# Four tiles for the attention's sums of x, an earlier copy of x into the output, and other banks at the borders of heads, in a one-core encoder block

## The chip, the cores and the metric

The kernel runs on one core of one Trainium2 chip. The metric is the device time of one execution in microseconds; the median of three runs is compared. PE is TensorE, DVE VectorE, ACT ScalarE, POOL GpSimd, SP the engine that issues nearly all DMAs. Numbers of lines (L748) are those of the kernel before.

## The reference

One encoder block on x of 1024 x 1024 (float32), with 16 learned meta tokens ahead of it:

```
u = rms_norm(h);  z = u @ w_in           # one projection, split into ten parts
branch A: bidirectional retention, 4 heads (dk 128, dv 256), chunks of 128,
          per-head norm, * silu(gate), @ w_ret_branch
branch B: windowed attention (+-128), 8 heads in 2 groups, rotary, meta keys,
          sink logit, * silu(gate), @ w_attn_branch
mix = sigmoid(g_r) * y_r + sigmoid(g_a) * y_a
out = h + rms_norm(mix @ w_out)          # meta rows dropped
```

## The kernel before

**Matmuls.** Every float32 product is three matmuls in the reduced type float32r: high times high, low times high, high times low (`mm3`, L79 to L81). Each operand is therefore split into a high part (a cast on ScalarE or GpSimd, `pool_hi` L92) and a low part (VectorE's subtraction `dve_lo`, L95). The large gate and branch products use a seven-product Strassen scheme (`Phase`), so sums and differences of quarters of x and of the weights are needed.

**Order of the work.** (1) Load x, split it, project q and k of head 0 (`qk0_mm`, over the k tiles), row squares of x on ScalarE (L377) for the norm; `normed` is the last of the instructions that make the row factors. `decay_table((h,))` (L248 to L250) makes head h's decay mask `DT`, with an exponential on ScalarE. (2) Four retention heads, `retention(h, fill)`: `stage1(c)` projects v of chunk c (`pv`), transposes k (`tr`) and makes the scores; `stage2(c)` makes the outputs of the forward scan (`pa`) and the states (`pkv`); then the backward scan runs over c from 8 down, with `finish(c)`, which transposes a normed output (`to`, L593), scales it on ScalarE into `ost` (L598) and stores it. (3) `attention()`: 32 chunks (2 groups, 16 blocks of 64 queries), `stage1` scores and softmax (`ps`, `p`), `stage2` transposes (`pt`), `stage3` values (`po`). (4) The phases z (gates), r and a (branch projections) and o (output projection, post norm, residual).

**What fills PE.** In a head's backward scan, `fill` takes steps of a list: the next head's q and k projection (`gen_qk`, 48 steps) and some steps of the "pre" products (`pe`, `gen_pre`; four steps make one product of 12 matmuls), namely (4, 4, 8) in heads 0, 1 and 2. There are seven fills of eight steps in such a head. A pre product (u, p) with p in `PRE[u]` is a product of phase z made ahead; its result goes to DRAM and is added in phase z. In the attention, `FILL[k]` gives how much of the remaining list is taken around chunk k, and `BEGUN` names, by the step of that list, helper work: loading and splitting weights (`half_w`, `pre_fetch`, `pre_sums`, `pre_parts`, `pre_low`) and the sums of x.

**Sums of x.** For eight steps q, `sum_fetch(q)` loads two tiles `xs` of 128 x 512 from x transposed (L748), `sum_scale(q)` scales them on ScalarE (L753), `sum_row(q)` forms four differences on VectorE in place (L760) and stores the two tiles to DRAM (L762). The two tiles are the only two buffers of their tag, so a step's fetch must wait for the store of the step before.

**Banks.** PSUM's eight banks are four groups: `pj` 3 (projections), `p1` 2 (`tr`, `to`, `rb`, `pt`), `p2` 2 (`pq` of head 0, `pkv`, `ps`), `p3` 1.

**The output.** Rows go out in tiles of 128. Rows 0, 1, 4 to 7 are added into `out` by an accumulating DMA of GpSimd, so x must lie there first: `x_to_out` copies x into `out` from DRAM to DRAM, 256 rows at a time, after chunks 4, 17 and 24 of the attention. Row tiles 2 and 3 come last; their x is loaded into SBUF (`xres`), added on VectorE (L1284), and a plain DMA on SP stores them. `final` is the last product, in two halves, each closed by `o_tail`.

**Scheduling.** The order within each engine is set by the framework from a simulated timeline; `tc.issue_after(i)` and `follow(...)` hold an instruction behind others.

Of the kernel before, what the change touches and what calls it, by code (L numbers as in the profile page):

```python
# [16 lines left out]
P = 128  # L17
KT = D // P
# [9 lines left out]
FILL = (((5, 4),) * 1 + ((5, 5),) * 1 + ((6, 4),) * 1 + ((4, 3),) * 1 + ((4, 5),) * 2 + ((4, 7),) * 1 + ((4,  # L28
        5),) * 1 + ((6, 4),) * 1 + ((5, 4),) * 1 + ((4, 3),) * 1 + ((4, 4),) * 1 + ((3, 5),) * 1 + ((4, 5),)
        * 1 + ((1, 4),) * 1 + ((6, 3),) * 1 + ((4, 5),) * 2 + ((4, 4),) * 1 + ((5, 4),) * 1 + ((3, 4),) * 1 +  # L30
        ((4, 3),) * 1 + ((4, 4),) * 2 + ((4, 2),) * 1 + ((4, 4),) * 1 + ((5, 4),) * 1 + ((3, 4),) * 1 + ((4,
        4),) * 1)
PRE = {u: (2, 3) if u > 5 else (2,) for u in range(2, 14)}
# [11 lines left out]
def block_kernel(ctx: ExitStack, tc: tile.TileContext, xT, x, meta, w_in, w_rb, w_ab, w_out, vecs, dec, sink,  # L45
# [106 lines left out]
    xm = wp.tile([P, KT, 2 * 32], R, name="xm")  # L152
# [45 lines left out]
    DT = ra.tile([P, NH, P], F32, name="DT")  # L198
# [69 lines left out]
    with tc.tile_pool(name="setup", bufs=1, reuse_waits="tile") as st:  # L268
# [119 lines left out]
    with tc.issue_after(rotated):  # L388
        decay_table((0,))
# [76 lines left out]
    def retention(h, fill):  # L466
# [122 lines left out]
        def finish(c):  # L589
            o = op[c - 1]  # L590
            to = p1(f"to{h}_{c}")
# [150 lines left out]
    def sum_fetch(q):  # L742

        k, c = q // 2, slice(256 * (q % 2), 256 * (q % 2) + 256)
        xsum[q] = {}
        for i in range(2):
            xsum[q][i] = t = aw.tile([P, 2, 256], F32, tag="xs", bufs=2, name=f"xs{i}{q}")
            nc.sync.dma_start(t, xT[4 * i + k, :, NM:T].rearrange("p (j t) -> p j t", j=2)[:, :, c])  # L748

# [114 lines left out]
    softmax, stored, last = [], [], {}  # L864
# [5 lines left out]
    with tc.issue_after(normed):  # L870
        evac_qk0(5)
    for h in range(NH):
        fill, drain = filler([gen_qk(h + 1), pieces(pre, (4, 4, 8)[h])] if h < 3 else [gen_ak(0), gen_ak(1), gen_aq(0, 0), gen_aq(0, 1), gen_aq(1, 0), gen_aq(1, 1)])
# [365 lines left out]
    rows, xres = {}, {}  # L1239
# [8 lines left out]
    def o_post(u, i, j, o, to=None):  # L1248
# [4 lines left out]
        if r not in rows:  # L1253
            rows[r] = (gp.tile([P, 3], F32, tag="ms2", bufs=4, name=f"ms2_{r}"), [], [])
            if u == 3:
                xres[i] = (lp if i else keep).tile([P, 4, 256], F32, tag="wr", bufs=2, name=f"xres{i}")
                xres[i] = xres[i].rearrange("p a b -> p (a b)")
                nc.sync.dma_start(xres[i], x[P * r:P * r + P])
# [3 lines left out]
        if u == 3:  # L1262
            nc.vector.tensor_tensor(to, o, pw[:, s], mul)
            o = xres[i]
# [14 lines left out]
    def o_out(r):  # L1279
        m2, parts, (m1,) = rows[r]  # L1280
        nc.gpsimd.tensor_tensor(m1, m1, mhalf[:, 0:1], ALU.pow)
        for s, to, o in parts:
            if r in (2, 3):
                nc.vector.scalar_tensor_tensor(to, to, m1, o[:, s], op0=ALU.mult, op1=ALU.add)  # L1284
                nc.sync.dma_start(out[P * r:P * r + P, s], to)
                continue
            nc.vector.scalar_tensor_tensor(to, o, m1, pw[:, s], op0=ALU.mult, op1=ALU.mult)
            nc.gpsimd.dma_start(out[P * r:P * r + P, s], to, accum_op=ALU.add)

    def o_tail(o, a):  # L1290
# [3 lines left out]
        nc.vector.tensor_tensor(o[:, s], o[:, s], pw[:, s], mul)  # L1294
        if a:
            parts.append((slice(0, 512), o, xres[1]))
# [53 lines left out]
    def attention():  # L1350
# [71 lines left out]
        def stage3(g, b):  # L1422
# [14 lines left out]
            if b % 2:  # L1437
                stored.append(nc.sync.dma_start(
                    oTa_d[4 * g:4 * g + 4, :, 64 * (b - 1):64 * (b + 1)].rearrange("e p t -> p e t"), oa[0]).ins)
# [55 lines left out]
        for k in range(len(chunks)):  # L1495
# [20 lines left out]
            if k in (4, 17, 24):  # L1516
                x_to_out({4: 0, 17: 4, 24: 6}[k])
# [6 lines left out]
             35: [(sum_scale, 3)], 37: [(sum_row, 3)], 40: [(sum_fetch, 4)], 45: [(sum_scale, 4)],  # L1524
# [124 lines left out]
```

## Time and profile before

| | |
|---|---|
| median of 3 runs | 1068.4 us (1066.32 to 1068.88) |
| the profiled execution | 1067.77 us, span 1066.0 us, mean granted clock 0.995 |
| PE busy | 1046.8 us (98%) |
| DVE, ACT, POOL busy | 849.2 (80%), 484.6 (45%), 212.4 (20%) |
| DMA | 190.36 MB, mean 179 GB/s |

The span runs from the first to the last instruction; the execution's own time is 1.8 us longer. A row of PE's waits names the instruction that waited, what it waited for, the total, the number of times and the longest. A row of windows gives busy time and started instructions of each engine in a stretch, then TensorE's granted clock (1.00 is full), the DMA engines' busy share and GB/s. In a timeline, `[0.61 <-ACT ost L598]` means that the engine was idle for 0.61 us before the instruction and what ended it. Matmuls overlap, so their times add to more than the span; counts per window are the better measure.

### The profile page before, as it was taken

The page shows a single profiled execution, that of the slowest core. Times are in us where ns is not written, and L with a number is a line of the kernel's source. Part 1 is how long each engine was busy: PE and PEld are TensorE (multiplying, and loading weights), DVE is VectorE, ACT ScalarE, POOL GpSimd, SP SyncE. Part 2 cuts the span into 40 slices and gives each one's busy share as a digit, 9 for nine tenths or more (in the row PEclk, how much of TensorE's full clock was granted, in tenths as well). Part 3 has the DMA queues.
Part 4 walks back from the last instruction along what each step waited for, and adds up shares of the span by engine and source line. Part 5 has one row for each costly group of instructions (what it writes and reads, how often), then busy time and mean ns, then how long its engine had stood idle before and what let it go on. Part 6 is the DMA issues. An engine that isn't in the chain of part 4 may idle for free.

```text
span 1066.0 us, 17137 instructions
## 1 busy us (share of the span) xinstructions
PE 1046.8 (98%) x5845; PEld 904.6 (85%) x5845; DVE 849.2 (80%) x1753; ACT 484.6 (45%) x1067; POOL 212.4 (20%) x270
## 2 busy tenths in 40 slices
PE   9999999999999999989999999999999999999997
PEld 7898999989998988877997888888888888787885
DVE  7787778768978548786768988998799799778765
ACT  5541442422411236565667545455456446333432
POOL 3324225134344224232210000000000000110032
PEclk9999999999999999999999999999999999999999
DMA  9321111203113427668668769899935746789464
GB/s 334 153 70 60 40 41 60 85 22 108 51 60 109 162 76 214 183 213 256 208 192 291 238 226 344 281 352 348 362 113 169 246 164 230 225 210 335 112 118 79
DMA packets 110632, 190.36 MB, mean 179 GB/s; under 512 B 11025, under 2 KB 50321, under 8 KB 109729
## 3 DMA queue, kind: packets, MB, share of 16 engines
q1 hardware_dynamic: 106944, 182.71, 51.4%
q0 software_dynamic: 3456, 6.29, 3.9%
q8 instruction: 46, 0.75, 0.3%
q14 instruction: 42, 0.34, 0.1%
q10 hardware_dynamic: 144, 0.27, 0.1%
HBM read 127.62 MB, written 62.40 MB: 178 GB/s over the span
## 4 chain that ended last, share of the span: by engine, by line
PE 94%; DVE 2%; DMA 1%; ACT 1%; issue 0%; SPq 0%; DVEq 0%; POOLq 0%; ACTq 0%
PE bz L80 8%; PE bz L81 8%; PE bz L79 8%; PE paq L80 3%; PE paq L79 3%; PE paq L81 3%; PE pv L79 3%; PE pv L81 3%; PE pv L80 3%; PE ba L80 2%; PE br L80 2%; PE br L79 2%; PE br L81 2%; PE ba L81 2%; PE ba L79 2%; PE bo L79 2%
## 5 line engine op out<-in xcount | busy, mean ns | idle before, releaser
L1232 POOL DMA_DIRECT2D mx_d<-c1a x4 | 3.7, 916 | 393.0 <-DVE c1a L1223 393.0
L81 PE MATMUL bz<-T,lhz 128*128 128x512 f32 x192 | 75.8, 395 | 0.0
L80 PE MATMUL bz<-T,llz 128*128 128x512 f32 x192 | 75.7, 394 | 0.0
L79 PE MATMUL bz<-T,lhz 128*128 128x512 f32 x192 | 75.2, 394 | 0.0
L79 PE MATMUL pv<-wh,big 128*128 128x256 f32 x256 | 73.0, 285 | 1.6 <-DVE vl L95 1.6
L80 PE MATMUL pv<-wh,big 128*128 128x256 f32 x256 | 73.1, 286 | 0.0
L81 PE MATMUL pv<-wl,big 128*128 128x256 f32 x256 | 73.0, 285 | 0.0
L80 PE MATMUL bz<-big,llz 128*128 128x512 f32 x176 | 69.7, 396 | 0.0
L81 PE MATMUL bz<-big,lhz 128*128 128x512 f32 x176 | 69.3, 394 | 0.0
L79 PE MATMUL bz<-big,lhz 128*128 128x512 f32 x176 | 68.8, 395 | 0.0
L1399 POOL TENSOR_SCALAR p<-p,den 128x352 f32<-128x352 f32 (+2 forms) x60 | 39.7, 674 | 107.7 <-DVE den L1392 82.8
L1389 ACT ACTIVATE p<-raw,nm 128x353 f32<-128x353 f32 (+2 forms) x64 | 36.1, 565 | 38.2 <-DVE nm L1386 37.9
L598 ACT ACTIVATE ost<-to,rnw 128x128 f32<-128x128 f32 x64 | 19.9, 364 | 73.2 <-PE to L593 58.3
L79 PE MATMUL paq<-big,wh 128*128 128x512 f32 x128 | 51.8, 405 | 0.0
L80 PE MATMUL paq<-big,wl 128*128 128x512 f32 x128 | 50.9, 398 | 0.0
L79 PEld LDWEIGHTS pv<-wh,big 128*128 128x128 f32 x256 | 48.9, 191 | 1.9 <-DVE vl L95 1.8
L81 PE MATMUL paq<-big,wh 128*128 128x512 f32 x128 | 50.4, 394 | 0.0
L81 PEld LDWEIGHTS pv<-wl,big 128*128 128x128 f32 x256 | 48.8, 191 | 0.1
L80 PEld LDWEIGHTS pv<-wh,big 128*128 128x128 f32 x256 | 48.8, 190 | 0.0
L80 PEld LDWEIGHTS bz<-T,llz 128*128 128x128 f32 x192 | 36.2, 188 | 8.5
L79 PEld LDWEIGHTS bz<-T,lhz 128*128 128x128 f32 x192 | 36.2, 188 | 8.4
L81 PEld LDWEIGHTS bz<-T,lhz 128*128 128x128 f32 x192 | 36.2, 188 | 8.4
(614 smaller groups left out, 3565.7 us busy)
## 6 DMA issues: line engine op xcount, KB each, us to landing
wrz<-in_w_in_dram SPq DMA_DIRECT2D x32, 512.0 KB, 6.0
wr<-in_w_in_dram SPq DMA_DIRECT2D x27, 512.0 KB, 4.0
e<-e SPq DMA_DIRECT2D x40, 256.0 KB, 4.8
we<-in_w_in_dram SPq DMA_DIRECT2D x16, 512.0 KB, 4.5
tg<-tg_d SPq DMA_DIRECT2D x32, 256.0 KB, 5.1
T<-preT SPq DMA_DIRECT2D x6, 1024.0 KB, 7.5
xt<-in_x_dram SPq DMA_DIRECT2D x8, 512.0 KB, 9.2
oTr_d<-ost SPq DMA_DIRECT2D x16, 256.0 KB, 2.1
```

Of the source, the lines that this page charges most:

```text
L79: nc.tensor.matmul(o, ah, bh, start=first, stop=False, **kw)
L80: nc.tensor.matmul(o, al, bh, start=False, stop=False, **kw)
L81: latest[:] = [nc.tensor.matmul(o, ah, bl, start=False, stop=last, **kw).ins]
L598: nc.scalar.activation(ost[0][:, e_, w0:w0 + P], to[:, P * e_:P * e_ + P], AF.Copy, scale=rnw[:, 2 * h + e_:2 * h + e_ + 1])
L1232: nc.gpsimd.dma_start(d, to, accum_op=ALU.add)
L1389: last["exp"] = nc.scalar.activation(p[:, 0:1 + wid], raw[e_][:, 0:1 + wid], AF.Exp, scale=-1.0, bias=nm_[:, e_:e_ + 1], accum_out=den[:, ...
L1399: nc.gpsimd.tensor_scalar(pt[e_][:, 0:wid], pt[e_][:, 0:wid], den[:, e_:e_ + 1], 1.0, op0=ALU.mult, op1=ALU.mult)
```

## The change

- **Sums of x.** Even steps keep the two `xs` tiles; odd steps use two other tiles, one in the slot of the decay masks `DT`, one in the slot of `xm` (the packed meta tokens).
- **Copies of x.** They leave the attention. In heads 0, 1 and 2, after the store of chunk 5 in `finish`, SP copies row tiles 0 to 2, 4 to 5 and 6 to 7.
- **Row tile 2** is no longer loaded. ScalarE scales it, and GpSimd's accumulating DMA adds it into `out`. Row tile 3 gets tiles of its own for the product with the post-norm weight, which was made in place.
- **Borders of heads.** `to` takes a bank of `p2` for c over 2. The pre steps in heads 0, 1 and 2 become (8, 8, 4), and unit 5 gets a second pre product, so that phase z has one product less.
- **First head.** In the first k step the products on the first half of x come ahead of the one on the second half of q. `decay_table((0,))` is placed behind `normed`.
- **`FILL` and `BEGUN`** are shifted by one or two at some chunks; the total of `FILL` at the last chunk is the same (254 with `START`).

```diff
-PRE = {u: (2, 3) if u > 5 else (2,) for u in range(2, 14)}
+PRE = {u: (2, 3) if u > 4 else (2,) for u in range(2, 14)}
...
         def qk0_mm(k):
-            for m0, a, b, o in outs:
-                mm3(o[:, 0:b - a], w0[0](k, m0, m0 + P), w0[1](k, m0, m0 + P), xh[k][:, a:b], xl[k][:, a:b],
-                    k == 0, k == KT - 1)
+            for i in (0, 2, 3, 1, 4, 5) if k == 0 else range(6):
+                m0, a, b, o = outs[i]
+                with follow(*(latest if k == 0 and i == 1 else ())):
+                    mm3(o[:, 0:b - a], w0[0](k, m0, m0 + P), w0[1](k, m0, m0 + P), xh[k][:, a:b], xl[k][:, a:b],
+                        k == 0, k == KT - 1)
...
     with tc.issue_after(rotated):
-        decay_table((0,))
         nc.vector.tensor_scalar(ms, ms, EPS, None, op0=ALU.add)
...
-            to = p1(f"to{h}_{c}")
+            to = (p2 if c > 2 else p1)(f"to{h}_{c}")
...
             if c % 2 == 1:
-                nc.sync.dma_start(
-                    oTr_d[2 * h:2 * h + 2, :, P * (c - 1):P * (c + 1)].rearrange("e p t -> p e t"), ost[0])
+                sent = nc.sync.dma_start(
+                    oTr_d[2 * h:2 * h + 2, :, P * (c - 1):P * (c + 1)].rearrange("e p t -> p e t"), ost[0]).ins
+                if h < NH - 1 and c == 5:
+                    with tc.issue_after(sent):
+                        r, e_ = ((0, 3), (4, 6), (6, 8))[h]
+                        nc.sync.dma_start(out[P * r:P * e_], x[P * r:P * e_])
...
-            xsum[q][i] = t = aw.tile([P, 2, 256], F32, tag="xs", bufs=2, name=f"xs{i}{q}")
+            xsum[q][i] = t = xs_tile[q % 2][i](f"xs{i}{q}")
...
+    xs_tile = [(lambda n, tag=tag: aw.tile([P, 2, 256], F32, tag="xs", bufs=2, name=n)) for tag in range(2)], [
+        lambda n: ra.tile([P, 2, 256], F32, tag="DT", bufs=1, name=n),
+        lambda n: wp.tile([P, 2, 256], F32, tag="xm", bufs=1, name=n)]
...
     with tc.issue_after(normed):
+        decay_table((0,))
         evac_qk0(5)
     for h in range(NH):
-        fill, drain = filler([gen_qk(h + 1), pieces(pre, (4, 4, 8)[h])] if h < 3 else [...])
+        fill, drain = filler([gen_qk(h + 1), pieces(pre, (8, 8, 4)[h])] if h < 3 else [...])
...
         for s, to, o in parts:
-            if r in (2, 3):
-                nc.vector.scalar_tensor_tensor(to, to, m1, o[:, s], op0=ALU.mult, op1=ALU.add)
+            if r == 3:
+                nc.vector.scalar_tensor_tensor(to, to, m1, xres[0][:, s], op0=ALU.mult, op1=ALU.add)
                 nc.sync.dma_start(out[P * r:P * r + P, s], to)
                 continue
-            nc.vector.scalar_tensor_tensor(to, o, m1, pw[:, s], op0=ALU.mult, op1=ALU.mult)
+            if r == 2:
+                nc.scalar.activation(to, to, AF.Copy, scale=m1)
+            else:
+                nc.vector.scalar_tensor_tensor(to, o, m1, pw[:, s], op0=ALU.mult, op1=ALU.mult)
             nc.gpsimd.dma_start(out[P * r:P * r + P, s], to, accum_op=ALU.add)
...
-            if k in (4, 17, 24):
-                x_to_out({4: 0, 17: 4, 24: 6}[k])
```

More of the change, by code (lines that the diff above doesn't have):

```diff
@@ L863, in block_kernel @@
     pre, fetched_w, parts = all_pre(), {}, {}
-    softmax, stored, last = [], [], {}
+    softmax, last = [], {}
     def marks(*names):
@@ L1238, in block_kernel @@
     pw = rbc[:, 0:D]
-    rows, xres = {}, {}
+    rows, xres = {}, []
     def o_head():
@@ L1254, in o_post @@
             rows[r] = (gp.tile([P, 3], F32, tag="ms2", bufs=4, name=f"ms2_{r}"), [], [])
[L1255 to L1258, printed above, removed]
+            if r == 3:
+                xres.append(lp.tile([P, 4, 256], F32, tag="wr", bufs=2, name="xres").rearrange("p a b -> p (a b)"))
+                nc.sync.dma_start(xres[0], x[P * r:P * r + P])
         m2, parts, _ = rows[r]
@@ L1533, in block_kernel @@
              105: [(pre_sums, 12)], 106: [(pre_parts, 12)], 107: [(pre_low, 12), (pre_fetch, 13)],
[L1534 to L1539 removed]
+             113: [(pre_sums, 13)], 114: [(pre_parts, 13), (pre_low, 13)]}
     i = attention()
```

41 lines of the change are left out of this document (20 added, 21 removed).

## The prediction

> **What bounds the kernel now.** I read the page's first part, then PE's waits, then the windows of 10 us around the places that those waits name, and last the timelines and the queue's waits there.
>
> ```profile
> span 1066.0 us, 17137 instructions
> PE 1046.8 (98%) x5845; PEld 904.6 (85%) x5845; DVE 849.2 (80%) x1753; ACT 484.6 (45%) x1067; POOL 212.4 (20%) x270
> ```
>
> PE is busy for 1046.8 of 1066.0 us, so the kernel is bound by TensorE, and all idle time of PE together is 19.2 us. A change that adds and removes no matmul can only touch that idle time, and the time in which PE ran at a lower clock. So the question is which stalls there are.
>
> ```profile
> PE pe L80 <- DVE wel L95: 2.2, 2, 1.4
> PE pt L1410 <- POOL p L1399: 1.8, 2, 1.5
> PE pv L79 <- DVE vl L95: 1.6, 1, 1.6
> PE idle L308 <- DVE ms L319: 1.5, 1, 1.5
> PE tr L500 <- ACT ost L598: 1.2, 2, 0.6
> PE pq L79 <- ACT big L335: 0.8, 1, 0.8
> ```
>
> These are PE's longest waits (total us, times, longest). They are few and each has a place: `pe` and `pt` in the attention, `pv` at the start of the first head, `tr` at two borders of heads, `pq` at the first step of the first projection. The windows give what each place costs:
>
> ```profile
> 110.00:120.00 10.00, 10.00 (x86) 9.73 (x84) 7.15 (x25) 2.41 (x10) 3.33 (x6) 1.00 0.12 44
> 120.00:130.00 10.00, 9.25 (x58) 8.26 (x58) 6.60 (x21) 4.94 (x17) 1.77 (x4) 0.83 0.11 39
> 260.00:270.00 10.00, 9.24 (x70) 8.13 (x69) 7.79 (x26) 3.98 (x14) 3.58 (x6) 1.00 0.17 56
> 460.00:470.00 10.00, 10.00 (x65) 8.95 (x64) 7.17 (x17) 6.03 (x14) 3.21 (x5) 1.00 0.73 230
> 470.00:480.00 10.00, 7.15 (x41) 5.55 (x39) 8.94 (x25) 7.14 (x20) 2.18 (x4) 1.00 0.70 225
> 480.00:490.00 10.00, 8.66 (x49) 7.20 (x47) 5.75 (x16) 4.29 (x12) 2.75 (x2) 1.00 0.69 210
> 490.00:500.00 10.00, 8.93 (x42) 7.56 (x43) 6.31 (x16) 5.22 (x15) 1.84 (x4) 0.83 1.05 306
> 500.00:510.00 10.00, 10.00 (x60) 8.69 (x59) 7.65 (x18) 7.00 (x17) 2.04 (x4) 1.00 0.77 238
> 600.00:610.00 10.00, 10.00 (x45) 8.09 (x44) 10.00 (x18) 5.73 (x11) 0.00 (x0) 1.00 0.50 162
> ```
>
> The columns are PE, PEld, DVE, ACT, POOL, then the granted clock, the DMA share and GB/s. From 470 to 500 us PE is idle for 2.85 + 1.34 + 1.07 = 5.26 us, and in the last of these windows the granted clock is 0.83, which is another 1.7 us (0.17 x 10). So 7.0 us are lost there, over a third of all that there is. At the border before head 1 (120 to 130) PE starts 58 matmuls where it started 86 in the window before; 28 fewer at 10/86 us are 3.3 us, of which the clock of 0.83 is 1.7. At the border before head 3 (260 to 270) it is 16 fewer, 1.9 us, at full clock.
>
> **Attention's sums: four tiles.** With two tiles, a fetch of a step overwrites what the step before must first write to DRAM.
>
> ```profile
> SPq L748 <- DMA xs<-xs: 5.8, 3, 2.6
> ACT xs L753 <- DMA xs<-in_xT_dram: 9.2, 4, 4.7
> DVE we L802 <- DMA we<-in_w_in_dram: 3.9, 2, 2.5
> 465.46 0.37 SPq L748 DMA_DIRECT2D xs<-in_xT_dram  x1
> 465.92 0.42 SPq L792 DMA_DIRECT2D we<-in_w_in_dram  x1
> 475.88 0.57 SPq L762 DMA_DIRECT2D xs<-xs  x1
> 479.97 0.37 SPq L748 DMA_DIRECT2D xs<-in_xT_dram  x1
> 484.76 0.72 ACT L753 ACTIVATE xs<-xs,vec 128x512 f32<-128x512 f32 x1 [4.73 <-DMA xs<-in_xT_dram]
> ```
>
> The three waits are those of 455 to 500 us. The last store leaves at 475.88, its fetch only at 479.97 when that store has landed, and ScalarE stands for 4.73 us until 484.76 with the exponentials of the softmax queued behind it. VectorE's sums, and the `pre_sums` that follow, stand behind ScalarE. The `we` load for the pre-product at 465.92 is queued on SP right behind such a blocked fetch (465.46), and VectorE waits 2.5 us for it. So all stalls from 470 to 500 have one source. With four tiles a fetch waits for the store of two steps before, which has landed by then, and SP is free. What is late next is VectorE: it does 8.94 + 5.75 + 6.31 = 21.0 us of work in these 30 us and must do it in 23, or 91%. I take 5.5 of the 7.0 us; the bounds are 1.5 (only the longest wait of PE goes) and 7.0. The two added tiles cost nothing: they lie in `DT` and `xm`, whose last readers are head 3's scores and the meta tokens' value projection, both before the first odd step. `FILL` and `BEGUN` shift pieces by one or two between chunks, and their total at the last chunk stays 254; I cost that at nothing, because PE's queue holds the same steps. If a chunk lacks its cover, the price is a stall of the size of those above, 0.7 to 1.5 us.
>
> **First head.**
>
> ```profile
> 36.15 0.18 ACT L377 ACTIVATION_READ_ACCUMULATOR xt<-xt 128x1 f32 x1
> 37.72 0.87 DVE L248 TENSOR_SCALAR dd<-tabt,lg 128x128 f32<-128x128 f32 x1
> 38.62 0.35 DVE L249 SCALAR_TENSOR_TENSOR dd<-tabt,lg,dd 128x128 f32<-128x128 f32 x1
> 39.01 0.31 ACT L250 ACTIVATE DT<-dd 128x128 f32<-128x128 f32 x1 [2.68 <-DVE dd L249]
> 41.43 0.17 DVE L390 TENSOR_SCALAR ms<-ms 128x9 f32<-128x9 f32 x1 [2.46 <-ACT xt L377]
> ```
>
> ScalarE has done seven row squares at 36.33, and then waits 2.68 us, with the last two squares behind the exponential of `decay_table((0,))`; VectorE waits for those squares until 41.43, and PE for `vl` (the 1.6 us above). Moved behind `normed`, the table lets the squares end about 2.7 us earlier, which is more than the stall. The table's 0.87 + 0.35 + 0.31 us then lie ahead of the first `sd`, beside PE's next value projections; without that cover they cost up to 1.2. The other order of the first k step gives PE nine matmuls on the half of x that is there, in place of the 0.8 us wait. That moves PE forward by 0.8 at all later points of the projection, where it has no wait. Together 2.4 at most; I take 2.2, with 1.0 as the lower bound.
>
> **Borders of heads.**
>
> ```profile
> 119.95 0.62 ACT L598 ACTIVATE ost<-to,rnw 128x128 f32<-128x128 f32 x2 [2.14 <-PE to L593]
> 120.63 0.33 PE L500 MATMUL tr<-ident,kr 128*128 128x128 f32 x1 [0.61 <-ACT ost L598]
> ```
>
> The next head's second `tr` needs a bank of `p1` that `to` still holds, until ScalarE has read it. With `to` in `p2` (for c over 2) `tr` goes on at once. What is late then is `khf`, ScalarE's next, so without other matmuls PE would still stand for about 0.5 us. Heads 0 and 1 now have 8 pre steps in place of 4: three matmuls each, 12 more, or 2.7 us by the 45 matmuls of the window at 600. The value projections that were used up before the border can lie in it. So I take 2.6 of the 3.3 us before head 1 (bounds 0 and 3.3), with the half-clock stretch in it. Head 2 loses four steps: before head 3 the new bank gains, the missing cover loses. I take 0, between a loss of 2.7 and a gain of 1.9. The product that moves into the retention costs no PE time net, being one product less in the z phase; its `pre_sums` and split lie on VectorE, which has 2.85 of 10 us free in the window at 110.
>
> On the clock: both windows with 0.83 come right at stalls of 0.61 us and of 1.5 us, but the stall of 1.6 us in the first head and the one before head 3 left it at full. So short stalls do lower the clock, not each time. The Trainium skill (TensorE: Matmul & The Clock Gate, section Why this matters for your kernels) says that the clock falls back after PE-idle gaps of over about 3 us; no run here shows a stall of that length before the lowered clock. By it neither of the two stretches comes from these stalls, and the sum would keep them.
>
> **x into the output, and the tail.**
>
> ```profile
> out_dram<-in_x_dram SPq DMA_DIRECT2D x3, 6.4
> 1057.63 0.75 DVE L1284 SCALAR_TENSOR_TENSOR u2o<-u2o,ms,xres 128x512 f32<-128x512 f32 x1
> 1058.30 0.29 PE L81 MATMUL bo<-T,lho 128*128 128x256 f32 x1
> 1059.28 0.41 DVE L1004 TENSOR_TENSOR u3o<-u3o,bo 128x256 f32<-128x256 f32 x1
> 1062.65 0.33 SPq L1285 DMA_DIRECT2D out_dram<-u3o  x1
> out_dram<-u2o POOLq DMA_DIRECT2D x1, 256.0 KB, 5.6
> out_dram<-u3o SPq DMA_DIRECT2D x1, 256.0 KB, 2.0
> ```
>
> The three copies of 1 MB (6.4 us each) leave the attention, where the DMA share is 0.7 to 1.05, for the retention, where it is 0.11 to 0.17; one is half as large again, about 10 us. On SP each is one issue behind the store of `ost`, and delays only the loads behind it. I cost them at nothing. At the end PE is done at 1058.6, but the last add starts at 1059.28, behind two scalings of row 2 on VectorE (0.7 each). On ScalarE these free VectorE, and the end comes 0.65 us earlier. But row 2 now goes out by GpSimd's accumulating DMA. Issued at about 1058.2, once row 2's factor and ScalarE's scaling are done, and 5.6 us long, it lands at 1063.8, near the last plain store (1062.65 - 0.65 + 2.0 = 1064.0). I take a gain of 0.4, with bounds of 0.65 and of a loss of 0.6. The Trainium skill (DMA: Bandwidth & Descriptors, section Anatomy of one DMA — SWDGE (gpsimd) path) has 2.0 us plus bytes over 436 GB/s for such a DMA, an estimate of 2.6 us here; the 5.6 us of the row are over twice that, and by the page the whole 0.65 would be gained.
>
> **The sum.** 2.2 + 2.6 + 0 + 5.5 + 0.4 = 10.7 us. Against it I set 0.9 us for stalls in the new order, half of one half-clock stretch of 1.7. That leaves 9.8. The profiled execution took 1067.77 us for its span of 1066.0, and is 0.6 below the median of 1068.4. 1067.8 - 9.8 = 1058.0.
>
> **Rivals.** *The clock stays.* The half-clock stretches fall on other short stalls, or have nothing to do with them. For it speaks that equal stalls did and did not lower the clock; against it, that both stretches lie at the two densest groups of stalls. Both stretches remain: 9.8 - 3.4 = 6.4, so 1061.4 us. This is also the outcome by the page's rule on gaps.
>
> *The attention stays bound.* The fetches come early, but VectorE, at 91%, becomes what PE waits for. Then the 5.5 shrink to the lower bound of 1.5: 1062.0 us. For it speaks the window at 470 with VectorE at 8.94; against it, that PE is at 10.00 in the windows at 460 and 500 with VectorE at 7.2 to 7.7.
>
> *No effect.* The stalls move to other borders and chunks, and what is saved is lost: 1066 to 1070 us.
>
> *Slower.* The copies hold the DMA engines while the next head's weights are queued behind them, and PE waits for the value projection. Together the copies are 3.5 MB, 22 us by the 6.4 us row. If the weights have no slack, 22.4 - 9.8 makes it 12.6 slower, 1080 us; it decides over the sign from a wait of 3.3 us at each of the three heads. Against it speak DMA shares of 0.11 and 0.12 around the border.
>
> **How the numbers follow.** What a measurement of this kernel can tell from no change is about 0.3%, or 3.2 us, so faster means under 1065.2. Chances: the forecast 0.52, the clock 0.17, VectorE 0.15, no effect 0.08, slower 0.08. The first three are faster: 0.84. The range begins at 1053.5, where nearly all bounds fall well (2.4 + 3.3 + 1.9 + 7.0 + 0.65 = 15.3 would be 1052.5), and ends at 1064.5, which takes in both weaker gains with a further 2.5 us lost before head 3; about 2 in 10 lie outside.
>
> **What would show it.** In the new profile PE's waits for `wel`, `p`, `vl` and `big` at the start should be gone, SP should have no wait of line `xs<-in_xT` for `xs<-xs`, and 470 to 500 should show PE at 10.00 and clock 1.00. At the border before head 1 the clock should be 1.00. Wrong would be: `xs` still waited for by ScalarE, a new wait of `pv` for a weight split in the retention, a clock of 0.83 at another border, or POOL's accumulate as the last to land.

## The result, and the profile after

The kernel after takes 1059.74 us in the median of six runs (1058.23 to 1061.35); the kernel before took 1065.82 beside it (1064.10 to 1068.88, its first three runs among the six). The ratio is 0.994, with a 95% interval from 0.992 to 0.9959: 6.1 us faster. The forecast was 1058.0 with a range of 1053.5 to 1064.5, so the time lies inside it. The profiled execution went from 1067.77 to 1059.64 us. That is 8.1 us, since before's profiled execution was 2 us above the median of its six runs.

The page of after, its first two lines, and the longest of PE's waits:

```profile
span 1057.8 us, 17121 instructions
PE 1039.7 (98%) x5845; PEld 899.5 (85%) x5845; DVE 850.9 (80%) x1753; ACT 485.9 (46%) x1068; POOL 216.5 (20%) x272
...
PE pe L80 <- DVE wel L95: 3.1, 3, 1.3
PE bz L79 <- ACT lhz L941: 2.0, 2, 1.5
PE pk L79 <- ACT big L337: 1.5, 1, 1.5
```

The waits for `vl`, for the softmax's `p` and for `ost` are gone. The wait for `wel` has grown, the one for `big` has become longer, and a wait in phase z is new. PE's idle time is 18.1 us where it was 19.2, yet the span is 8.2 us shorter. So most of the time came out of busy time: matmuls counted as busy while they were held up or ran at half clock. That is why counts and first and last starts say more here than busy shares.

The windows of after around the places of the prediction (PE, PEld, DVE, ACT, POOL, clock, DMA share, GB/s):

```profile
120.00:130.00 10.00, 10.00 (x85) 9.84 (x85) 7.44 (x23) 5.71 (x19) 1.86 (x4) 1.00 0.15 52
260.00:270.00 10.00, 10.00 (x84) 9.70 (x83) 8.68 (x26) 4.01 (x13) 3.87 (x7) 1.00 0.10 31
450.00:460.00 10.00, 9.03 (x57) 7.83 (x56) 9.69 (x24) 7.02 (x17) 2.94 (x4) 1.00 0.75 248
460.00:470.00 10.00, 9.52 (x62) 8.27 (x60) 9.93 (x26) 7.71 (x22) 3.13 (x5) 1.00 0.71 232
470.00:480.00 10.00, 9.20 (x50) 7.93 (x51) 8.49 (x24) 6.63 (x17) 2.47 (x4) 1.00 0.83 254
480.00:490.00 10.00, 10.00 (x60) 8.92 (x60) 7.18 (x16) 6.72 (x16) 2.54 (x4) 1.00 0.70 207
490.00:500.00 10.00, 10.00 (x61) 8.76 (x60) 6.00 (x15) 4.61 (x14) 1.09 (x2) 1.00 0.64 180
500.00:510.00 10.00, 9.14 (x56) 8.00 (x55) 7.76 (x16) 6.08 (x16) 2.63 (x4) 1.00 0.79 225
```

At the two borders PE now starts 85 and 84 matmuls, nearly as many as in an undisturbed window (86); it started 58 and 70. From 470 to 500 it is idle for 0.8 us, not 5.3, and the clock is full. But PE has lost 1.0 us at 450 and 0.5 at 460, with VectorE at 9.69 and 9.93, and 0.9 at 500; in these three windows before had no idle time. Over all of 450 to 510 the idle time falls from 5.3 to 3.1 us. The window of before at 450:

```profile
450.00:460.00 10.00, 10.00 (x63) 9.11 (x63) 9.76 (x26) 6.20 (x18) 3.88 (x5) 1.00 0.53 162
```

The view of one tile gives the first and last start of its matmuls, and so the ends of the stages. Before:

```profile
L166 PE MATMUL pv<-wh,xm x32: 275/276/283, 30.8 to 243.3; 128*48 128x256 f32 x32
L79 PE MATMUL pkv<-vh,khf x32: 276/285/582, 46.6 to 290.6; 128*128 128x256 f32 x28, 16*128 16x256 f32 x4
L79 PE MATMUL ps<-kTh,aqh x64: 255/322/495, 385.6 to 558.5; 128*128 128x352 f32 x48, 128*128 128x208 f32 x8, 128*128 128x288 f32 x8
L79 PE MATMUL bo<-big,lho x64: 388/395/502, 979.5 to 1052.0; 128*128 128x512 f32 x64
```

and after:

```profile
L166 PE MATMUL pv<-wh,xm x32: 276/276/362, 29.5 to 239.5; 128*48 128x256 f32 x32
L79 PE MATMUL pkv<-vh,khf x32: 274/283/382, 43.5 to 286.8; 128*128 128x256 f32 x28, 16*128 16x256 f32 x4
L79 PE MATMUL ps<-kTh,aqh x64: 255/322/344, 379.1 to 547.5; 128*128 128x352 f32 x48, 128*128 128x208 f32 x8, 128*128 128x288 f32 x8
L79 PE MATMUL bo<-big,lho x64: 388/395/502, 969.9 to 1042.6; 128*128 128x512 f32 x64
```

Each stage is the change from one row to the next. In a row, three durations in ns (least, median, most) stand ahead of the first and the last start. The first value projection comes 1.3 earlier, and the first state product `pkv` a further 1.8. The attention starts 6.5 earlier, so the borders gave 3.4, although a product of 12 matmuls (2.7 us) was put into them. The attention's scores end 11.0 earlier: 4.5 more. The output phase starts only 9.6 earlier: 1.4 was lost in between, where a product had been taken out. The span is 8.2 shorter: 1.4 went after that row.

These are rows of one execution each. How far they can be trusted is seen from kernels that share the code of a stage: in the six with the heads of after, the way from the first `pkv` to the attention takes 335.6 to 335.7 us, and in the four with its attention, the way from the first to the last scores (`ps`) takes 167.9 to 169.5 us. The start repeats less well: the kernel with four tiles alone (below) begins as before does, and has its first value projection at 29.3. So the first 1.3 us need not be the change's.

Nearly all of the loss after the last row lies behind PE. Timelines of after, and its DMA issues with the median time to landing:

```profile
1048.89 0.29 PE L81 MATMUL bo<-T,lho 128*128 128x256 f32 x1
1049.22 0.42 DVE L1014 TENSOR_TENSOR u3o<-u3o,bo 128x256 f32<-128x256 f32 x1
out_dram<-pw POOLq DMA_DIRECT2D x2, 256.0 KB, 6.2
out_dram<-pw SPq DMA_DIRECT2D x2, 256.0 KB, 3.9
```

VectorE's last add now starts 0.04 us behind PE's end, as planned; it was 0.69. But the span ends 8.6 us after PE, where it was 7.4: the plain stores on SP land after 3.9 us, not 2.0, beside the new accumulating DMA. This profile is the worst case. After and eight of the kernels below have this end, and their spans end 7.5 to 8.6 us after PE (8.1 in the median), with stores of 2.8 to 3.9 us; the four kernels that add row 2 on VectorE have 7.3 to 7.5. So the loss is 0.1 to 1.3 us, 0.7 in the median.

### The profile page after: what moved, and what is told of

Same layout as the page of the kernel before. It is cut to its first block, busy times and chain, and to the rows that moved or that the text cites. A ratio compares the mean times of both kernels' runs of the same rounds, so it can differ in the third digit from the quotient of the medians.

```text
span 1057.8 us, 17121 instructions
## 1 busy us (share of the span) xinstructions
PE 1039.7 (98%) x5845; PEld 899.5 (85%) x5845; DVE 850.9 (80%) x1753; ACT 485.9 (46%) x1068; POOL 216.5 (20%) x272
## 4 chain that ended last, share of the span: by engine, by line
PE 81%; DVE 8%; DMA 6%; ACT 2%; issue 2%; SPq 0%; DVEq 0%; POOLq 0%; ACTq 0%
PE bz L80 5%; PE bz L79 5%; PE bz L81 5%; PE pv L81 3%; PE pv L79 3%; PE pv L80 3%; PE paq L80 3%; PE paq L79 3%; PE paq L81 3%; PE bo L80 2%; PE bo L79 2%; PE bo L81 2%; PE ba L80 2%; PE ba L79 2%; PE ba L81 2%
## 5 line engine op out<-in xcount | busy, mean ns | idle before, releaser
L79 PE MATMUL bz<-big,lhz 128*128 128x512 f32 x172 | 67.8, 397 | 2.0 <-ACT lhz L941 2.0
L81 PE MATMUL bz<-big,lhz 128*128 128x512 f32 x172 | 67.7, 394 | 0.0
L1403 ACT ACTIVATE p<-raw,nm 128x353 f32<-128x353 f32 (+2 forms) x64 | 36.1, 566 | 43.8 <-DVE nm L1400 41.8
```

What stands on the lines that cost most here:

```text
L79: nc.tensor.matmul(o, ah, bh, start=first, stop=False, **kw)
L81: latest[:] = [nc.tensor.matmul(o, ah, bl, start=False, stop=last, **kw).ins]
L1403: last["exp"] = nc.scalar.activation(p[:, 0:1 + wid], raw[e_][:, 0:1 + wid], AF.Exp, scale=-1.0, bias=nm_[:, e_:e_ + 1], accum_out=den[:, ...
```

## The experiments

Each kernel was timed in five rounds beside the kernel before on the same chip. "After" in a diff is the changed kernel.

**Row tile 2 as before.** After, with row 2 on VectorE, its x loaded, a plain store:

```diff
-                        r, e_ = ((0, 3), (4, 6), (6, 8))[h]
+                        r, e_ = ((0, 2), (4, 6), (6, 8))[h]
...
-            if r == 3:
-                nc.vector.scalar_tensor_tensor(to, to, m1, xres[0][:, s], op0=ALU.mult, op1=ALU.add)
+            if r in (2, 3):
+                nc.vector.scalar_tensor_tensor(to, to, m1, (xres if r == 3 else x2)[0][:, s], op0=ALU.mult, op1=ALU.add)
```

> The changed kernel, with row tile 2 as it was before: x loaded, scaled and added on VectorE, a plain store by SP; the copies of x cover row tiles 0 to 1, 4 to 5 and 6 to 7. Theory (the accumulating DMA of row 2 shares the DMA engines with the last two plain stores, which took 3.9 us to land in place of 2.0): the stretch from the last matmul's end to the end of the span goes back from 8.6 us to 7.4, the last stores land in 2.0 to 2.3 us, and the kernel is about 1.2 us faster than the changed one (0.993 of the kernel before, against 0.994). Rival (the longer end has another source, such as the in-place product that got a tile of its own): the stretch stays at 8.6, or grows by the 0.65 us of VectorE's scalings to 9.2.

1058.38 us; ratio 0.9923 [0.9907, 0.9939], the best of all runs. Its last matmul, its last add and its stores:

```profile
1048.82 0.29 PE L81 MATMUL bo<-T,lho 128*128 128x256 f32 x1
1049.81 0.41 DVE L1014 TENSOR_TENSOR u3o<-u3o,bo 128x256 f32<-128x256 f32 x1
out_dram<-pw SPq DMA_DIRECT2D x4, 256.0 KB, 2.5
```

PE ends at the same point, and the last add is 0.6 later, yet the span ends at 1056.4, 1.4 earlier, since the stores land in 2.5 us. The theory holds in its direction: the change's part for row 2 is a loss. Its size is less sure: 1.4 us between these two profiles, 1.8 by the ratios, whose intervals overlap, and 0.7 by the median of the nine ends above.

**Four tiles alone**, on the kernel before:

```diff
-            xsum[q][i] = t = aw.tile([P, 2, 256], F32, tag="xs", bufs=2, name=f"xs{i}{q}")
+            xsum[q][i] = t = xs_tile[q % 2][i](f"xs{i}{q}")
...
```

> The kernel before, with the two further tiles for the sums of x and nothing else. Theory of the prediction (all stalls from 470 to 500 us have the fetch that waits for the store as their one source): SP waits no longer for a store before a fetch, 470 to 500 shows PE at 9.5 or more in each window, and the kernel is 4 to 5.5 us faster than the kernel before (0.995 to 0.996). Rival (VectorE is at 91% or more and takes the fetch's place): SP's wait goes all the same, but PE still idles 3 us or more there, and the gain is 1 to 2.5 us.

1065.09 us; 0.9982 [0.9969, 0.9995]. The rival's 1 to 2.5 us. The tile view, the windows, and SP's waits of this kernel:

```profile
L79 PE MATMUL ps<-kTh,aqh x64: 255/321/342, 384.2 to 553.3; 128*128 128x352 f32 x48, 128*128 128x208 f32 x8, 128*128 128x288 f32 x8
```

```profile
470.00:480.00 10.00, 8.24 (x47) 6.65 (x45) 8.91 (x27) 6.57 (x18) 3.04 (x4) 1.00 0.79 231
490.00:500.00 10.00, 8.73 (x51) 7.11 (x50) 6.83 (x16) 5.91 (x15) 1.10 (x2) 1.00 0.91 275
```

```profile
SPq L748 <- DMA xs<-xs: 5.7, 6, 2.6
```

The attention is 3.8 us shorter than in before's profile, 1.7 of it the clock; the 2.1 that are left agree with the median, as far as a stage that repeats within 1.6 us can tell. ScalarE has no wait for `xs` left, where it had 10.0 us in the whole of before, and PE's waits for the softmax's `p` fall from 1.8 to 0.3 us. But the fetches on SP still wait for stores (5.7 us in 6 waits, 10.0 in 7 in before), against the theory and the rival alike, and PE's waits for `wel` stay at 2.2. The first of them, at 476, still has a fetch ahead of it: it waited 2.6 us for a store until 463, with a load of `we` queued behind it. The second, at 497, comes long after the last fetch, so it has another source. In after the same wait has 4.0 us, the longest 1.3:

```profile
SPq L753 <- DMA xs<-xs: 4.0, 6, 1.3
```

**The sums' differences on GpSimd**, in after, to see whether VectorE is what binds the attention now:

```diff
-            nc.vector.tensor_tensor(x[o], x[a], x[b], ALU.subtract)
+            nc.gpsimd.tensor_tensor(x[o], x[a], x[b], ALU.subtract)
```

> The changed kernel, with the four differences of each sum of x (128 x 256, 0.42 us each on VectorE) done by GpSimd. Theory (in the attention VectorE, busy for 9.7 to 9.9 of 10 us from 450 to 470, has become what PE waits for, in place of the fetches): VectorE's share there falls below 9, PE's waits for wel (3.1 us in all) fall below 1.5, and the kernel is 1 to 2 us faster than the changed one (0.992 to 0.993 of the kernel before). Rival (GpSimd takes about 0.75 us for each and the softmax's scaling is queued behind them on it): PE waits for pt on p instead, and it is the same or up to 2 us slower.

1060.01 us; 0.9947 [0.9929, 0.9964]: no gain. PE's waits and a window:

```profile
PE pt L1424 <- POOL p L1413: 2.6, 3, 1.2
PE pe L80 <- DVE wel L95: 1.9, 2, 1.6
```

```profile
460.00:470.00 10.00, 8.11 (x53) 6.90 (x51) 8.39 (x23) 7.23 (x20) 9.84 (x8) 1.00 0.45 138
```

VectorE falls from 9.93 to 8.39. After's two waits for `wel` at 457 and 471, 2.3 us together, are gone, so there VectorE's load was what PE waited for. The wait that is left, at 484, stands behind a load of `we` for which VectorE waited 4.1 us. But GpSimd is now full in that window, and the softmax's scaling on it is late by as much.

**The copies of x back in the attention**, in after:

```diff
-                if h < NH - 1 and c == 5:
-                    with tc.issue_after(sent):
...
+            if k in (4, 17, 24):
+                r, e_ = {4: (0, 3), 17: (4, 6), 24: (6, 8)}[k]
```

> The changed kernel, with the copies of x into the output issued in the attention again, after chunks 4, 17 and 24 (row tiles 0 to 2, 4 to 5, 6 to 7). The prediction costed the move at nothing. Theory: within 0.5 us of the changed kernel (0.994). Rival (at DMA shares of 0.7 to 1.05 in the attention the copies hold up the weights of the pre products): PE's waits for wel grow by 1 us or more behind a copy, and it is 1 to 2 us slower (0.995 to 0.996).

1060.49 us; 0.9952 [0.9936, 0.9969], 0.0012 above after's ratio, within both intervals. PE's wait for `wel` is 2.9. The heads take 335.8 us from the first `pkv` to the attention and the attention 168.5 from its first to its last scores, against 335.6 and 168.4 in after. The place of the copies is worth nothing that these runs can tell.

**`FILL` and `BEGUN` as before**, in after (the two tables replaced, nothing else).

> The changed kernel, with FILL and BEGUN as before. The prediction costed their shifts at nothing, with 0.7 to 1.5 us if a chunk lacks its cover. Theory: the same within 1 us of the changed kernel (0.993 to 0.995 of the kernel before), and PE's wait for wel stays at 3 us. Rival (the shifts belong to the four tiles, since they move loads and sums to where SP and VectorE are free now): waits of pt or ps return, 2 us or more slower (0.996 or more).

1062.85 us; 0.9967 [0.9949, 0.9985]. The ratio is the rival's, with an interval that overlaps after's. The profile shows one small new wait of PE (`weh`, 0.9 us), and SP's waits of fetches for stores of `xs` back at 6.6 us, the longest 2.8. The attention takes 169.8 us from its first to its last scores, little over the 167.9 to 169.5 with the tables of after, and the profiled execution took 1059.43 us, less than after's, because its end came 7.6 us behind PE. The median comes from other executions: the five up to 1061.66 us have a mean granted clock of 0.997 to 0.999, the six from 1062.85 to 1067.97 of 0.993 to 0.995. So the two tables seem worth up to 3 us in the median by the clock; why the old ones would lower it more often, and whether that is chance, stays open.

**The decay table alone**, on the kernel before:

```diff
     with tc.issue_after(rotated):
-        decay_table((0,))
...
     with tc.issue_after(normed):
+        decay_table((0,))
```

> The kernel before, with head 0's decay table behind the row factors and nothing else. Theory: PE's wait of 1.6 us for vl in the first head is gone, the first pkv comes 1.8 us earlier, and the gain is 1.6 to 1.9 us (0.998 to 0.9985). Rival: the table's VectorE work holds up the first scores, and PE stalls by 0.5 to 1.2 us between 45 and 52 us, so that 0.4 to 1 us are left.

1063.22 us; 0.9981 [0.997, 0.9993]. The tile view:

```profile
L166 PE MATMUL pv<-wh,xm x32: 275/277/280, 29.8 to 239.7; 128*48 128x256 f32 x32
L79 PE MATMUL pkv<-vh,khf x32: 276/283/388, 43.8 to 287.0; 128*128 128x256 f32 x28, 16*128 16x256 f32 x4
```

From the first `pv` to the first `pkv` it is 14.0 us, as in after, where it was 15.8. So 1.8 us are the table's, and the wait for `vl` is gone. The first `pv` came 1.0 earlier here too, and 1.5 in four tiles alone, both with the first k step as before: the new order has no part in the 1.3 of after that could be seen.

**All products on the second half of x held**, in after:

```diff
-                with follow(*(latest if k == 0 and i == 1 else ())):
+                with follow(*(latest if k == 0 and i in (1, 4, 5) else ())):
```

> The changed kernel, with the two k products on the second half of x in the first k step held back like the one of q. In the changed kernel the scheduler put them ahead of the low parts, and PE waited 1.5 us for the second half of x there. Theory: PE has nine matmuls to do first, the wait falls to 0.3 us or less, and the first value projection starts 1 to 1.4 us earlier at the same clock; about 1.2 us faster than the changed kernel (0.993). Rival: x of the next k steps is what the projection waits for, the wait moves to the second or third k step, and nothing is gained.

1059.55 us; 0.9938 [0.9921, 0.9954], the same as after. PE's timeline from 5 to 10 us has a single wait left:

```profile
9.23 0.47 PE L79 MATMUL pq<-big,w 128*128 128x512 f32 x1 [0.60 <-ACT big L337]
```

In after the change held only the product on the second half of q. The scheduler put the first matmuls of `pk` on the second half ahead of the low parts, and PE waited 1.51 us there. With these held too, the wait moves to the second k step, which needs its x.

**The pre steps back to (4, 4, 8)**, with one product of unit 5 (the bank of `to` stays):

```diff
-PRE = {u: (2, 3) if u > 4 else
+PRE = {u: (2, 3) if u > 5 else
...
-pieces(pre, (8, 8, 4)[h])
+pieces(pre, (4, 4, 8)[h])
```

> The changed kernel, with the pre steps of heads 0 to 2 as before, (4, 4, 8), and unit 5 with one pre product, so that phase z has the product again. Theory (z is bound by the DMA engines from 640 to 740 us, and the product taken out of it came back as 3.5 us of stalls on weights): the stalls on line L941 go, z is no longer than in the changed kernel (264 us from its first to its last matmul), the retention is 2.7 us shorter, and PE stalls again for 0.5 to 1.5 us in all at the borders: 1 to 2.5 us faster than the changed kernel's 1059.7 (0.992 to 0.993 of the kernel before). Rival (the filler is worth what the prediction gave it): the stalls at the borders before heads 1 and 2 return with 1 to 3 us and the half-clock stretch, and it is 1 to 3 us slower (0.995 to 0.997).

1062.31 us; 0.9964 [0.9949, 0.9978]: 2.6 us slower than after by the ratios.

```profile
L79 PE MATMUL ps<-kTh,aqh x64: 256/321/344, 381.4 to 550.5; 128*128 128x352 f32 x48, 128*128 128x208 f32 x8, 128*128 128x288 f32 x8
```

The attention starts 2.3 us later than in after, though 2.7 us less work lies ahead of it: the cover is worth 5.0 us there. Phase z, in the rows of its `bz` (this kernel, then after), and a window of 20 us of after with a row of its timeline:

```profile
L79 PE MATMUL bz<-big,lhz x176: 387/395/507, 554.7 to 818.7; 128*128 128x512 f32 x176
L79 PE MATMUL bz<-big,lhz x172: 387/395/504, 551.7 to 815.6; 128*128 128x512 f32 x172
```

```profile
660.00:680.00 20.00, 18.53 (x80) 14.72 (x79) 19.78 (x33) 11.03 (x19) 0.00 (x0) 1.00 0.89 285
```

```profile
676.91 0.62 ACT L941 CAST lhz<-wrz 128x512 fp32r<-128x512 f32 x1 [3.11 <-DMA wrz<-in_w_in_dram]
```

Phase z takes 263.9 us in after and 264.0 here, with 12 matmuls more, 2.7 us of work. In this window after starts 80 matmuls where 88 go into 20 undisturbed us, so 8 or 1.8 us are missing; from 700 to 720 it starts 82. Phase z has one product less to do while the same weights come in at a DMA share of 0.9 to 1.0, and PE waits for them. So the product that was moved out of z saved next to nothing there.

**The bank of `to` as before**, in after:

```diff
-            to = (p2 if c > 2 else p1)(f"to{h}_{c}")
+            to = p1(f"to{h}_{c}")
```

> The changed kernel, with all of to in p1 again, and the more filler kept. Theory of the prediction (the bank makes tr wait, filler closes what is left): tr waits again for ost, 0.6 us at each of two or three borders, at times with a half-clock stretch; 1.2 to 2.5 us slower than the changed kernel (0.995 to 0.9965). Rival (filler alone is enough, since value projections are left to lie in the wait): no wait of tr over 0.2 us, and the same time within 0.5 us.

1066.30 us; 1.0001 [0.9988, 1.0014]. The whole gain is gone, more than was expected. The tile view, windows at two borders, PE's wait for the bank, and a row of its timeline in phase z:

```profile
L79 PE MATMUL ps<-kTh,aqh x64: 255/322/343, 384.6 to 553.3; 128*128 128x352 f32 x48, 128*128 128x208 f32 x8, 128*128 128x288 f32 x8
```

```profile
120.00:130.00 10.00, 9.66 (x76) 8.94 (x75) 6.95 (x22) 6.24 (x21) 1.21 (x3) 1.00 0.16 54
260.00:270.00 10.00, 9.37 (x71) 8.36 (x71) 8.27 (x27) 4.43 (x15) 3.12 (x6) 1.00 0.46 159
```

```profile
PE tr L501 <- ACT ost L599: 1.0, 2, 0.5
```

```profile
684.81 0.80 PE L79 MATMUL bz<-big,lhz 128*128 128x512 f32 x1 [2.87 <-ACT lhz L941]
```

The attention starts 5.5 us later than in after, at full clock: 9 and 13 matmuls are missing at the two borders. The wait that is named for it is 1.0 us. The rest are gaps too short for a row of their own; that they come from `to`, its scaling on ScalarE, `tr` and `khf` taking turns in two banks is argued, not shown. A further part of this profile lies in phase z: after a wait of 2.87 us for `lhz` the matmul takes 0.80 us, twice its usual 0.39 (the median of its group), at half clock. Phase z takes 267.3 us with it, and the execution 2.1 more than the median.

Measured from the first `pkv` (at 43.6 us in this kernel and at 43.3 in the one above), so with the start and the table taken off, the way to the attention is 341.0 us here, 338.1 in the one above, and 335.6 in after. Before has 339.0, with a half-clock stretch in it. The kernel with the decay table alone has before's bank and cover and no such stretch at a border, so it is the better base:

```profile
L79 PE MATMUL ps<-kTh,aqh x64: 255/322/499, 382.0 to 553.5; 128*128 128x352 f32 x48, 128*128 128x208 f32 x8, 128*128 128x288 f32 x8
```

From 43.8 to 382.0 it takes 338.2 us. Against it the borders gave 5.3 us in after (2.6 shorter, and 2.7 of added work), nothing with the cover alone (2.8 longer, 2.7 added) and 0.1 with the bank alone. Neither works without the other. The likely reason is that the bank lets the next head's transposes and the old head's outputs pass each other, and that the pre steps are what PE then does in between. That is not shown: the framework orders each engine anew for every edit, and a part may come from another order.

**The extra product from unit 2 instead of unit 5**, in after:

```diff
-PRE = {u: (2, 3) if u > 4 else (2,)
+PRE = {u: (2, 3) if u > 5 or u == 2 else (2,)
```

> The changed kernel, with the additional pre product taken from unit 2 in place of unit 5. The product then leaves phase z at about 590 us, where the DMA share is 0.5 to 0.8, and not at 650, ahead of the stretch with shares of 0.93 to 1.03. Theory (the stalls come from too little PE work just where the DMA engines are full): they go or shrink below 1 us, and the kernel is 2 to 3.5 us faster than the changed one (0.991 to 0.992). Rival (z as a whole has too few matmuls for its transfers, wherever one is taken out): the stalls stay at 2.5 to 3.5 us, no gain.

1061.45 us; 0.9961 [0.9945, 0.9976]. Its wait in phase z is smaller (1.4 us for `llz`, none for `lhz`), but the attention starts 1.7 us later than in after, and why it does is open.

**The extra product from unit 14.** This kernel takes the product out of the last pair of phase z, whose end sets when quarters of x are loaded anew; the refill comes one product early, and the last products of z read other data.

```diff
-PRE = {u: (2, 3) if u > 4 else (2,) for u in range(2, 14)}
+PRE = {u: (2, 3) if 5 < u < 14 else (2,) for u in (2, 3, 4, 5, 14, *range(6, 14))}
```

> The changed kernel, with the additional pre product taken from unit 14 in place of unit 5; all else is the same. Theory (phase z is bound by the DMA engines between 640 and 740 us, so that a product less ahead of it returns as three stalls of 1.8, 1.4 and 0.4 us on weights): unit 14 comes behind that stretch, the three stalls go, and the kernel is 2.8 to 3.5 us faster than the changed one (0.991 of the kernel before). Rival (the stalls come from what starts earlier as a whole, since phase z begins 11 us earlier against its loads): the stalls stay, 0 to 0.5 us.

1065.59 us; 0.9987 [0.9971, 1.0002]. Because of the early refill it says nothing on the question.

**Row 2 on ScalarE and GpSimd, with a plain store**, on the kernel with row 2 as before:

```diff
             if r in (2, 3):
-                nc.vector.scalar_tensor_tensor(to, to, m1, (xres if r == 3 else x2)[0][:, s], op0=ALU.mult, op1=ALU.add)
+                if r == 2:
+                    nc.scalar.activation(to, to, AF.Copy, scale=m1)
+                    nc.gpsimd.tensor_tensor(to, to, x2[0][:, s], ALU.add)
+                else:
+                    nc.vector.scalar_tensor_tensor(to, to, m1, xres[0][:, s], op0=ALU.mult, op1=ALU.add)
```

> The kernel after, with x of row tile 2 loaded and a plain store of it on SP, as before the change, but scaled by ScalarE and with x added by GpSimd, so that VectorE has neither scaling, and no accumulating DMA goes out with the last stores. With row 2 on VectorE and a plain store, the end came 7.3 us after the last matmul and the ratio was 0.9923; with ScalarE and the accumulating DMA 8.6 us and 0.994. Theory: the change's loss at the end is the accumulating DMA alone, and ScalarE in VectorE's place is a gain that it hides. VectorE's last add then follows PE at once as in the kernel after (there 0.05 us behind PE, else 0.7), and the stores land in 2.0 to 2.5 us: 6.7 to 7.0 us behind the last matmul, a ratio of about 0.9918. Rival: GpSimd's two adds (1.5 us each by its other rows of 128x512) stand ahead of the power of row 3 and delay it by what VectorE saves or more: 7.3 to 8.3 us, a ratio of 0.9923 to 0.933+0.06=0.993.

1059.72 us; 0.9943 [0.9927, 0.9959]: slower than with row 2 on VectorE. Its timeline and DMA issues:

```profile
1050.00 0.42 DVE L1014 TENSOR_TENSOR u3o<-u3o,bo 128x256 f32<-128x256 f32 x1
1050.00 2.97 POOL L1298 TENSOR_TENSOR pw<-pw,xres 128x512 f32<-128x512 f32 x2 [0.84 <-ACT pw L1297]
1050.34 1.52 DVE L1276 TENSOR_TENSOR pw<-c5o,rbc 128x512 f32<-128x512 f32 x1
1051.12 0.29 PE L81 MATMUL bo<-T,lho 128*128 128x256 f32 x1
1051.78 1.48 DVE L1312 TENSOR_TENSOR pw<-u3o,rbc 128x256 f32<-128x256 f32 x1
1053.18 0.41 DVE L1014 TENSOR_TENSOR u3o<-u3o,bo 128x256 f32<-128x256 f32 x1
out_dram<-pw SPq DMA_DIRECT2D x4, 256.0 KB, 2.1
```

The span of 1059.7 ends 8.3 us behind PE, the rival's time. The stores land in 2.1 us in the median of four again, so the 3.9 in after belongs to the accumulating DMA beside them. But the last add starts 1.8 us behind PE: VectorE's products with the post-norm weight take 1.52 and 1.48 us while GpSimd's adds run, and 0.69 and 0.42 in the other kernels. The rival had the delay on GpSimd's own queue; it is on VectorE. The Trainium skill (SBUF — State Buffer, section Who interferes with whom) says that a VectorE instruction with two inputs in SBUF contends with a GpSimd instruction that reads SBUF, over a shared pair of ports, and calls that pair an exclusive lock. The rows agree: the add `u3o<-u3o,bo`, with one input in PSUM, keeps its 0.42 us at 1050.00.

## Why the prediction held, and where its steps did not

The direction and the range were right, and the forecast of 1058.0 was 1.7 us too low. The saving in the profile, 8.1 us for a predicted 9.8, is near; but it was set against one profiled execution that was itself longer than the median of its kernel, and the medians differ by 6.1. That the forecast came so near is in part luck: an overestimate of the attention and of the tail stands against borders that gave more than their term. (One reading was also too high: the 7.0 us lost from 470 to 500 are 31%, not over a third, of the 19.2 us of idle time and 3.4 of clock.) The steps fared as follows.

**First head: 2.2 predicted.** The larger part, the wait for `vl`, was right: the table alone gives 1.8 us. The other part, 0.8 for the new order of the first k step, failed: the wait for x did not go but moved. It is 1.5 us in after and 0.6 to 1.5 in the other kernels with this order, against 0.8 to 1.3 with the old one. The step said that nine matmuls lie in its place; the diff held back only one of the three products on the second half, and with all three held x of the next k step was late instead. PE waits for the arrival of x there in either order.

**Borders: 2.6 + 0 predicted, with a product moved in at no cost.** The stretch from the first `pkv` to the attention became 3.4 shorter with 2.7 more work in it, so the borders themselves were under-sized: 6.1 against before's profile with its half-clock stretch, 5.3 against a kernel without one. That bank and cover depend on each other was said for the first border, but the sum treated them as additive, and took nothing for the border before head 3, which is as full as the other in after.

**The moved product: "no PE time net".** This step failed. It was paid in the retention and not earned back in phase z, where weights set the pace: 263.9 us with the product taken out, 264.0 with it. The z phase was not looked at for its own bound. Together with the borders the two errors nearly cancel: 3.4 less the 1.4 lost up to the output phase is 2.0, for 2.6 predicted. That is luck.

**Attention: 5.5 predicted.** The mechanism was right in part: ScalarE's waits for `xs` are gone, 470 to 500 is nearly full, the clock is 1.00. The size was too large: 4.5 between the rows of the two profiles, with 1.7 of clock in it; the four tiles alone give 1.9 in the medians. The step that failed is that a store of two steps before "has landed by then, and SP is free": with the tiles alone SP's fetches still wait 5.7 us, up to 2.6 at once, and 4.0 in after. Nor did all stalls have one source: with the tiles alone PE's wait for `wel` at 497 comes after the last fetch, and in after idle time came up at 450 and 500. VectorE did become what PE waits for, as the rival had it: at 9.69 and 9.93 from 450 to 470, with `wel` up from 2.2 to 3.1. The rival's price of 1062.0 was too high, but its mechanism holds part of the 5.5, and moving the sums to GpSimd only changed which engine is late.

**Tail: a gain of 0.4 predicted.** The sign was wrong. The step costed the accumulating DMA by its own landing and took the plain stores' 2.0 us as given. Beside the accumulate they took 2.8 to 3.9 in nine kernels, and the change lost 0.1 to 1.3 us, with 1.2 in after's own profile. By the Trainium skill's figure (DMA: Bandwidth & Descriptors, section Anatomy of one DMA — SWDGE (gpsimd) path), an estimate of 2.6 us, the whole 0.65 would have been gained; the rows of 4.8 to 6.2 us in the nine and 5.6 before decide against it.

**Costed at nothing.** The copies of x are free as far as these runs can tell: 0.2 us or less in the stages, 1.3 by the ratios with overlapping intervals. The tables `FILL` and `BEGUN` may not be: up to 3 us in the median, mostly in executions of lower clock that no profile shows.

**The clock.** The rival that both half-clock stretches stay did not come true in after's profile, whose windows of 10 us are all at full clock until PE is done. Other executions seem to have them still: of after's six, two have a mean granted clock of 0.995, that of before's profile, and these are the two longest (1061.17 and 1061.35 us); the other four, at 0.998 and 0.999, took 1058.23 to 1059.83. The rule of the Trainium skill on gaps (TensorE: Matmul & The Clock Gate, section Why this matters for your kernels) would have kept them. In four tiles alone the stretch at 120 to 130 stayed and the one at 490 to 500 went, though a stall of 0.8 us stayed there. In phase z after's stall of 1.5 us had no stretch behind it, and the same wait, 1.8 us long in the kernel with row 2 on GpSimd, had one. So the stretches seen here begin at stalls, but a stall alone does not settle that one comes.

The version with the lowest median is after with row tile 2 as it was before: 1058.38 us.

## What to carry to other kernels

Look at the bound of the place from which work is taken, not only of the place to which it goes: a product moved out of a phase that waits for its weights saves nothing. Of two small edits at one place, one that frees a resource and one that gives the engine work to do with it, each can be worth nothing alone and both together several microseconds, so they are tried together. At the end of a kernel cost each DMA beside the others that are in flight, and set a sum worked out on one profiled execution against the median of more than three runs. A stage that several profiled kernels share shows how much one profile can be trusted: here the heads repeat within 0.1 us and the end of the kernel only within 1.1.

## What the runs showed of the hardware

- The last two plain stores of 256 KB landed in 2.0 to 2.1 us in the three kernels that end as before does, and in 2.8 to 3.9 beside two accumulating DMAs of the same size, which took 4.8 to 6.2 (nine kernels).
- A product of two SBUF operands on VectorE took 1.5 us in place of 0.69 (128x512) or 0.42 (128x256) while GpSimd added two SBUF operands.
- The clock fell in whole stretches in these profiles. Windows of 1 us of before, behind stalls of 1.51 and 0.77 us:

```profile
491.00:492.00 1.00, 0.30 (x2) 0.00 (x0) 1.00 (x2) 1.00 (x5) 0.00 (x0) 0.87 0.82 306
492.00:493.00 1.00, 0.93 (x2) 0.83 (x3) 0.11 (x3) 1.00 (x4) 0.74 (x2) 0.50 0.82 243
```

  The clock goes to 0.50 behind a window of 1 us with 0.3 us of matmul work. The window of 10 us had 0.83 in the mean, which is 3.4 us at half clock and 1.7 us lost. In the kernel with the old bank the lowered clock came behind a stall of 2.87 us, the longest of PE in these traces; what one of 3 us or more does, no run here shows.
